# Input projection of a hybrid decoder block: weight groups of 512 columns in a ring of one group, in place of 256 columns in a ring of two

## Chip, cores and metric
One Trainium2 chip; the kernel runs on one of its cores. The metric is the device time of one execution in microseconds (us), lower is better.

## What is computed
A decoder block for 2,048 tokens of width 1,024, all in float32: a mixer (two attention groups fed by one input projection), cross-attention into 256 memory rows, a mixture of 16 experts, and a last norm. Only the input projection and what reads it matter here:

```python
# h = rms_norm(x, mix_norm): (1, 2048, 1024); w_in: (1024, 3096)
fq, fk, fv, ff, gq, gk, gv, gg, ga = jnp.split(h @ w_in, offsets, axis=-1)
# widths         512 512 512  8  256 256 512 512 16
fox = forgetting_attention(fq, fk, fv, ff + b_forget)         # 8 heads x 64
log_a = log_sigmoid(ga @ w_alpha_up + b_alpha) / 16
gla = gla_chunked(gq, gk, gv, log_a)                          # 4 heads, chunks of 64 tokens
gla = rms_norm(gla) * silu(gg)
y = concat(rms_norm(fox), gla) @ w_out
```

## The kernel before
**Precision.** A product of float32 operands is three matmuls of float32r parts: `split` (lines 64 to 72) makes a high part on ACT (line 68, or line 71 with a scale) and a low part on DVE (line 69 or 72), and `mm3` (lines 88 to 92) runs high by high (L90), high by low (L91) and low by high (L92) into one PSUM bank.

**Stage 1** (`stage1`, lines 129 to 290). The tokens are four chunks of 512. `prenorm` loads and normalises a chunk, `turn` transposes it on PE (L205) and splits it into xh and xl, which stay in SBUF for the whole stage. The columns of w_in are taken in groups. `group` (lines 140 to 148) loads a group in 8 parts (one for each 128 of the 1,024 rows) through the staging tile w1s, a ring of 4, and splits each, scaled by mix_norm, into w1r, a ring of 16: two groups of 256 columns. Two kinds of product use a group:

- `ttype` (lines 159 to 167), the transposed product: 128 columns of the group stand in the array, 512 tokens of a chunk move. 8 parts by 3 matmuls fill one bank, which is evacuated by ACT and DVE in turn (`evac`, L155 and L157) and stored by SP (L167).
- `ntype` (lines 169 to 180), the token-major product: 128 tokens stand, the group's 256 columns move. 8 parts by 3 matmuls, evacuated by `evac` or, for GG, by ACT with Silu (L179), and stored by SP (L180).

Both draw on the tile ps_mm (three banks) and on the output tile o1 (two buffers). The groups come in this order: GQ and GK (two groups, transposed, lines 234 to 264, chunk by chunk, with the transposition of the next chunk and a narrow product of 24 matmuls, `narrow`, at each chunk's end); GG and GV (two groups each, token-major, 16 token tiles to a group, lines 266 to 271); FV (two groups, token-major) and FQ, FK (two groups each, transposed, four heads to a group), in the generator `rest` (lines 273 to 287). The steps of `rest` are interleaved with those of the GLA recurrence (`gla`, lines 328 to 454), half a step of GLA per unit of main work (`interleave`, lines 34 to 44): a tile counts 2.6 units when token-major and 5.2 when transposed.

**Order of the work.** The program is written as above, but the order on each engine is made by a scheduler when the program is built: it takes what is ready by its own estimate of times, so that matmuls of different tiles, of GLA and of the transpositions may run in another order than in the text. Each engine then runs its list strictly in order. SP's list holds both the loads and the stores of this stage.

**After stage 1.** `stage2` (lines 457 to 640) is the forgetting attention, head by head. `prep` (lines 468 to 491) loads a head's queries (L474), keys (L475), running sums cr (L477) and values (L482) from DRAM, for head 0 through POOL's queue, and splits queries and keys (ACT L486 and L489, DVE L487, POOL L490); `scores` starts with L506 on PE. Its tiles take SBUF space that stage 1 used, and each waits for the tiles it covers. Stage 3a later loads w_xq with `load_w` (lines 643 to 650): 8 parts of 128 rows by 512 columns through wst, a ring of 2, split in the same way.

Of the kernel before, what the change touches and what calls it, by code (L numbers as in the profile page):

```python
# [33 lines left out]
def interleave(main, side, ratio):  # L34
    """emits side's steps among main's, `ratio` of side's per unit of main's; then what is left"""
    due, live = 0.0, True
    for w in main:
        due += w * ratio
        while live and due > 0:
            step = next(side, None)  # L40
            live = step is not None
            due -= step or 0.0
    for _ in side:
        pass


def skip(gen, n):
    """gen, after n empty steps"""
    for _ in range(n):
        yield  # L50
    yield from gen


class Trunk:
# [9 lines left out]
    def split(self, hi, lo, src, scale=None):  # L64
        """hi + lo = src (* scale), each exact in a float32r"""
# [8 lines left out]
    def rstd(self, out, ss, mul, pool, eps=EPS, tag=""):  # L74
        """out = (ss * mul + eps) ** -0.5"""
# [19 lines left out]
    def consts(self):  # L95
# [8 lines left out]
        # -1e30 above the diagonal (row q, column k > q)  # L104
# [5 lines left out]
        with self.tc.tile_pool(name="vrows", bufs=1) as rp, self.tc.tile_pool(name="ps_c", bufs=1, space=PSUM) as pp:  # L110
# [10 lines left out]
            # blank lists for the routing  # L121
# [7 lines left out]
    def stage1(self):  # L129
# [3 lines left out]
        with tc.tile_pool(name="xT", bufs=1) as xp, tc.tile_pool(name="w1", bufs=2) as wp, \  # L133
                tc.tile_pool(name="ps1", bufs=2, space=PSUM) as pp:
            xh, xl = zip(*[[xp.tile([128, KT, 512], F32R, name=f"x{n}{c}") for n in "hl"] for c in range(4)])
            # the narrow columns: forget logits at 0..7, GLA gate inputs at 32..47
# [3 lines left out]
            def group(c0):  # L140
                ws = []
                for k in range(KT):
                    st = wp.tile([128, 256], F32, name="w1s", bufs=4)
                    nc.sync.dma_start(st, w_in[k * 128:(k + 1) * 128, c0:c0 + 256])
                    w = wp.tile([128, 2, 256], F32R, name="w1r", bufs=16)
# [13 lines left out]
            def ttype(ws, m, c, dst):  # L159
                """rows m*128.. of the group's transposed product, tokens of chunk c"""  # L160
# [8 lines left out]
            def ntype(ws, i, dst, func=None):  # L169
                c, j = divmod(i, 4)  # L170
                ps = pp.tile([128, 256], F32, name="ps_mm", bufs=3)
# [3 lines left out]
                o = wp.tile([128, 256], F32, tag="o1", name="o1", bufs=2)  # L175
# [6 lines left out]
            with tc.tile_pool(name="xin", bufs=2) as ip, tc.tile_pool(name="psx1", bufs=2, space=PSUM) as px:  # L182
                xn = [[] for _ in range(4)]

                def prenorm(c):
                    """load and normalise chunk c"""
# [11 lines left out]
                def turn(c):  # L198
                    """chunk c transposed: yields after each bank"""
# [10 lines left out]
                def narrow(c):  # L210
# [6 lines left out]
                    # c: the running sum of log sigmoid(forget logit)  # L217
# [16 lines left out]
                gq, gk = group(GQ), group(GK)  # L234
                prenorm(1)
                for c in range(4):
                    cs = slice(c * 512, (c + 1) * 512)
                    tn = turn(c + 1) if c < 3 else iter(())
                    for m in range(2):
                        for n, ws in enumerate((gq, gk)):  # L240
                            ttype(ws, m, c, self.gqk_d[m, n, :, cs])
                            for _ in range(2):
                                next(tn, None)
                            if (c, m, n) == (0, 0, 0):
                                z = ip.tile([128, 8 * S // 128 + 1, 5], I32, name="zl", bufs=1)
                                nc.gpsimd.memset(z, 0)
                                # a blank entry's token is past the end in the fourth column
# [18 lines left out]
            for c0, dst in ((GG, self.gg_d), (GV, self.gv_d)):  # L266
                for g in range(2):
                    ws = group(c0 + g * 256)
                    for i in range(NT):
                        ntype(ws, i, dst[i * 128:(i + 1) * 128, g * 256:(g + 1) * 256],  # L270
                              AF.Silu if c0 == GG else None)

            def rest():
                for g in range(2):
                    ws = group(FV + g * 256)
                    for i in range(NT):
                        ntype(ws, i, self.fv_d[i * 128:(i + 1) * 128, g * 256:(g + 1) * 256])
                        yield 2.6
                for b, c0 in ((0, FQ), (8, FK)):
                    for g in range(2):  # L280
                        ws = group(c0 + g * 256)
                        for c in range(4):
                            for m in range(2):
                                h = b + 4 * g + 2 * m
                                dst = self.fqk_d[h:h + 2, :, c * 512:(c + 1) * 512].rearrange("h d s -> (h d) s")
                                ttype(ws, m, c, dst)
                                yield 5.2
# [6 lines left out]
    def gla_masks(self):  # L294
        nc, c = self.nc, self.cpool
        # GLA: of a 64-token chunk, which (key s, query t) a level of blocks of 2h settles:
        # s in a block's first half, t in its second; 0: s <= t within blocks of 8
# [30 lines left out]
    def gla(self, gp, pp):  # L328
# [19 lines left out]
        for g in range(S // G):  # L348
# [3 lines left out]
            for p in range(2):  # L352
# [9 lines left out]
                # log decay, summed within chunks (16 times the reference's, taken off in the exps)  # L362
# [29 lines left out]
                # scores within chunks, level by level  # L392
# [13 lines left out]
                # within blocks of 8: factors of both signs about the block's middle, bounded as each  # L406
                # step's decay is held at exp(-17), under a float32's resolution beside the diagonal
# [10 lines left out]
                # between the halves of blocks of 2h, about the first half's end  # L418
# [28 lines left out]
                # the queries' factor 1/8 is in here: (o / 8) / sqrt(mean(o^2) / 64 + eps)  # L447
# [9 lines left out]
    def stage2(self):  # L457
        nc, tc = self.nc, self.tc
        with tc.tile_pool(name="fx", bufs=1, reuse_waits="tile") as fp, \
                tc.tile_pool(name="psx", bufs=2, space=PSUM, reuse_waits="tile") as pp:  # L460
            vs, heads, n_evac = {}, {}, [0]
            # in the order in which the last head lets go of them, for the stage that follows
# [5 lines left out]
            def prep(h):  # L468
# [9 lines left out]
                # [q hi; q lo] over 8 against [k hi; k hi] and [k lo; k lo]  # L478
# [14 lines left out]
            def scores(u):  # L493
                """exp(s - max) of head h's query block, and its sums: yields after each bank"""
# [26 lines left out]
            def values(u0, u1):  # L521
                """the outputs of two query blocks, transposed, in the array's two column halves:
                yields after each bank"""
# [1082 lines left out]
```

## Time and profile before

| | |
|---|---|
| runs | 2484.33, 2485.76, 2489.12 us |
| median | 2485.76 us |
| span of the profiled execution, first to last instruction | 2482.5 us |
| from that span to the runs shown | 1.8 (lowest) to 6.6 us (highest) |
| PE busy | 2368.5 us (95%) |
| PEld busy (weight loads) | 2022.0 us (81%) |
| DVE, ACT, POOL busy | 1444.0, 1087.4, 451.5 us |
| mean granted clock of TensorE | 0.979 |
| matmuls | 17,849 |

The profile gives the profiled execution its span only; its own time in the sense of the runs is not listed apart, so it stands beside the runs as in the fourth line. Times within the profile count from the span's start. PE is TensorE's matmuls, PEld its weight loads, which overlap them; the duration of a matmul includes its way through the array, so that one begins before the one ahead has ended. A name such as `ps_mm<-xh,w1r` reads: the tile written, from the tiles read. `L90` is line 90; the helpers' lines (68 to 72, 90 to 92, 155, 157) serve many callers, so the tile's name tells which. In brackets stands how long the engine was idle ahead of an instruction, and who released it. SPq, POOL with DMA_DIRECT2D, and so on are transfers being issued.

### The profile page before, as it was taken

Reading aid. Unit: us, or ns where it says so; the run is one execution under the profiler, and the core shown is the slowest. Engines: PE = TensorE matmul, PEld = TensorE weight load, DVE = VectorE, ACT = ScalarE, POOL = GpSimd, SP = SyncE. Lnnn points to the kernel's source line nnn. Section 1 sums busy time; section 2 is a strip of 40 time slices with the busy share of each in tenths; the row PEclk is TensorE's granted clock in tenths of the full one; section 3 lists DMA queues with packets and bytes.
Section 4 is the critical chain, followed back from the end, with each engine's and each line's share of the span. In section 5 each row is a group of like instructions: output and inputs, shape, how many; then the busy total and the mean of one; then the engine's idle time right before and its main releaser. Section 6 shows DMA issues by size and latency. Waiting matters only on the chain. (4 is left out here: it accounts for less than half of the span.)

```text
span 2482.5 us, 46191 instructions
## 1 busy us (share of the span) xinstructions
PE 2368.5 (95%) x17849; PEld 2022.0 (81%) x17849; DVE 1444.0 (58%) x4096; ACT 1087.4 (44%) x2438; POOL 451.5 (18%) x460
## 2 busy tenths in 40 slices
PE   7999999999999999999999999999599999999996
PEld 5799999877776777777778888888499989889995
DVE  5321145455447777767542236656567868768775
ACT  6322123233236666666431035544344545454542
POOL 1000012122122222211100000111323233223231
PEclk9999999999999999999999999999799999999998
DMA  5232222332274223200174421111478888879783
GB/s 174 70 93 82 71 75 88 97 92 89 74 195 103 66 72 80 66 27 10 39 260 143 140 104 45 59 53 52 152 227 258 239 274 255 255 236 270 263 246 110
DMA packets 275218, 328.99 MB, mean 133 GB/s; under 512 B 30774, under 2 KB 223088, under 8 KB 271921
## 3 DMA queue, kind: packets, MB, share of 16 engines
q1 hardware_dynamic: 243968, 223.79, 28.9%
q0 software_dynamic: 31024, 102.20, 14.1%
q8 instruction: 141, 2.31, 0.4%
q14 instruction: 85, 0.69, 0.1%
HBM read 251.88 MB, written 84.30 MB: 135 GB/s over the span
## 5 line engine op out<-in xcount | busy, mean ns | idle before, releaser
L90 PE MATMUL gu<-xTh,wer 128*128 128x288 f32 x1024 | 305.4, 303 | 0.5 <-ACT xTh L68 0.5
L91 PE MATMUL gu<-xTl,wer 128*128 128x288 f32 x1024 | 304.7, 298 | 0.0
L92 PE MATMUL gu<-xTh,wer 128*128 128x288 f32 x1024 | 303.8, 297 | 0.0
L69 DVE TENSOR_TENSOR wer<-wes,wer 128x1024 fp32r<-128x1024 f32 x192 | 232.2, 1220 | 35.3 <-ACT wer L68 34.4
L68 ACT ACTIVATE wer<-wes 128x1024 fp32r<-128x1024 f32 x192 | 197.7, 1052 | 108.8 <-PE yd L92 42.5
L90 PE MATMUL ps_mm<-w1r,xh 128*128 128x256 f32 x768 | 219.3, 286 | 0.0
L91 PE MATMUL ps_mm<-w1r,xh 128*128 128x256 f32 x768 | 218.7, 285 | 0.0
L92 PE MATMUL ps_mm<-w1r,xl 128*128 128x256 f32 x768 | 217.9, 284 | 0.0
L90 PEld LDWEIGHTS gu<-xTh,wer 128*128 128x128 f32 x1024 | 193.9, 190 | 3.7 <-ACT xTh L68 0.9
L92 PEld LDWEIGHTS gu<-xTh,wer 128*128 128x128 f32 x1024 | 194.9, 190 | 1.8
L91 PEld LDWEIGHTS gu<-xTl,wer 128*128 128x128 f32 x1024 | 194.9, 190 | 1.5
L518 ACT ACTIVATE sc<-sc,m 128x1024 f32<-128x1024 f32 (+2 forms) x192 | 170.9, 892 | 51.2 <-DVE m L515 51.0
L536 PE MATMUL pt<-ident,sc 128*128 128x128 f32 x1088 | 177.8, 289 | 7.3 <-DVE rc L556 3.7
L529 PE MATMUL po<-t,v 128*64 128x128 f32 x2176 | 178.3, 287 | 0.0
L529 PEld LDWEIGHTS po<-t,v 128*64 128x64 f32 x2176 | 124.1, 138 | 49.4 <-issue 21.7
L536 PEld LDWEIGHTS pt<-ident,sc 128*128 128x128 f32 x1088 | 126.6, 145 | 45.2 <-issue 28.3
L506 PE MATMUL ps_s<-L,R 128*128 128x512 f32 (+2 forms) x320 | 140.4, 440 | 15.8 <-DVE m L510 11.1
L90 PE MATMUL ps_mm<-xh,w1r 128*128 128x512 f32 x384 | 153.8, 403 | 0.0
L92 PE MATMUL ps_mm<-xh,w1r 128*128 128x512 f32 x384 | 153.0, 398 | 0.0
L91 PE MATMUL ps_mm<-xl,w1r 128*128 128x512 f32 x384 | 152.8, 398 | 0.0
L90 PEld LDWEIGHTS ps_mm<-w1r,xh 128*128 128x128 f32 x768 | 147.2, 192 | 3.8 <-issue 1.9
L510 DVE CUSTOM_DVE_ANT_0 sc<-ps_s,cr,m 128x512 f32<-128x512 f32 (+2 forms) x192 | 124.3, 647 | 44.4 <-PE ps_s L507 31.6
(405 smaller groups left out, 5780.3 us busy)
## 6 DMA issues: line engine op xcount, KB each, us to landing
wes<-in_w_expert_down_dram SPq DMA_DIRECT2D x64, 512.0 KB
wes<-in_w_expert_gate_dram SPq DMA_DIRECT2D x62, 512.0 KB
wes<-in_w_expert_up_dram SPq DMA_DIRECT2D x62, 512.0 KB
yr_d<-ye SPq DMA_DIRECT2D x32, 512.0 KB
w1s<-in_w_in_dram SPq DMA_DIRECT2D x96, 128.0 KB
xt<-in_x_dram SPq DMA_DIRECT2D x16, 512.0 KB
fqk_d<-o SPq DMA_DIRECT2D x32, 256.0 KB
h_d<-x POOLq DMA_DIRECT2D x16, 512.0 KB
```

The source lines that it names most:

```text
L68: nc.scalar.activation(hi, src, AF.Copy)
L69: nc.vector.tensor_tensor(lo, src, f32(hi), OP.subtract)
L90: mm(ps, ah, bh, start=start, stop=False)
L91: mm(ps, ah, bl, start=False, stop=False)
L92: mm(ps, al, bh, start=False, stop=stop)
L506: nc.tensor.matmul(ps[:, :w], R[:, qs], L1[:, ks], start=True, stop=False)
L510: nc.vector.tensor_tensor_reduce(out=sc[:, ks], in0=ps[:, :w], in1=cr[:, ks], scale=1.0, scalar=m[:, i - 1:i] if i else -3e38, op0=OP.subt ...
L518: nc.scalar.activation(sc[:, cs], sc[:, cs], AF.Exp, bias=m[:, 4:5], accum_out=u["l"][:, j:j + 1])
L529: nc.tensor.matmul(po[half * 64:half * 64 + 64], v[:, kb, d], t[:, i], start=kb == 0, stop=kb == qb + half)
L536: nc.tensor.transpose(pt[:, i], (u0, u1)[half]["P"][:, kb * 128:(kb + 1) * 128], self.ident)
```

## The change
A group becomes 512 columns wide. w1s goes from four buffers of 256 columns to two of 512, and w1r from 16 slots of 2 x 256 to 8 of 2 x 512: the same bytes, but one group. GQ and GK, which are neighbours in w_in, become one group. The token-major product moves 512 columns into a bank, so that GG, GV and FV are one group each with 16 tiles, not two with 16 each. FQ and FK are one group each, with the four pairs of heads inside the loop over the chunks. The diff also drops comments and docstrings, which are left out here.

```diff
@@ group, ntype
-                    st = wp.tile([128, 256], F32, name="w1s", bufs=4)
-                    nc.sync.dma_start(st, w_in[k * 128:(k + 1) * 128, c0:c0 + 256])
-                    w = wp.tile([128, 2, 256], F32R, name="w1r", bufs=16)
+                    st = wp.tile([128, 512], F32, name="w1s", bufs=2)
+                    nc.sync.dma_start(st, w_in[k * 128:(k + 1) * 128, c0:c0 + 512])
+                    w = wp.tile([128, 2, 512], F32R, name="w1r", bufs=8)
...
-                ps = pp.tile([128, 256], F32, name="ps_mm", bufs=3)
+                ps = pp.tile([128, 512], F32, name="ps_mm", bufs=3)
...
-                o = wp.tile([128, 256], F32, tag="o1", name="o1", bufs=2)
+                o = wp.tile([128, 512], F32, tag="o1", name="o1", bufs=2)
@@ stage1
-                gq, gk = group(GQ), group(GK)
+                gqk = group(GQ)
...
-                        for n, ws in enumerate((gq, gk)):
-                            ttype(ws, m, c, self.gqk_d[m, n, :, cs])
+                        for n in range(2):
+                            ttype(gqk, 2 * n + m, c, self.gqk_d[m, n, :, cs])
...
-                for g in range(2):
-                    ws = group(c0 + g * 256)
-                    for i in range(NT):
-                        ntype(ws, i, dst[i * 128:(i + 1) * 128, g * 256:(g + 1) * 256],
-                              AF.Silu if c0 == GG else None)
+                ws = group(c0)
+                for i in range(NT):
+                    ntype(ws, i, dst[i * 128:(i + 1) * 128], AF.Silu if c0 == GG else None)
@@ rest
-                for g in range(2):
-                    ws = group(FV + g * 256)
-                    for i in range(NT):
-                        ntype(ws, i, self.fv_d[i * 128:(i + 1) * 128, g * 256:(g + 1) * 256])
-                        yield 2.6
+                ws = group(FV)
+                for i in range(NT):
+                    ntype(ws, i, self.fv_d[i * 128:(i + 1) * 128])
+                    yield 5.2
                 for b, c0 in ((0, FQ), (8, FK)):
-                    for g in range(2):
-                        ws = group(c0 + g * 256)
-                        for c in range(4):
-                            for m in range(2):
-                                h = b + 4 * g + 2 * m
+                    ws = group(c0)
+                    for c in range(4):
+                        for m in range(4):
+                            h = b + 2 * m
```

## Rows read from the trace of the kernel before

**Rows 1.** Busy time of each engine in six stretches (us from the span's start): GQ and GK; GG and GV; FV beside GLA; FQ and FK beside GLA; the step to the attention. Columns: the stretch, its length, busy us (and instructions) of PE, PEld, DVE, ACT and POOL, the granted clock, the DMA share and GB/s.
```profile
22.97:145.00 122.03, 122.03 (x575) 95.29 (x575) 54.87 (x130) 51.46 (x116) 0.00 (x0) 1.00 0.33 100
145.00:331.00 186.00, 186.00 (x1549) 185.74 (x1548) 28.82 (x88) 34.30 (x81) 0.18 (x1) 1.00 0.24 74
331.00:467.00 136.00, 136.00 (x1503) 124.44 (x1502) 76.08 (x194) 48.53 (x167) 31.47 (x36) 1.00 0.30 87
467.00:724.00 257.00, 257.00 (x2109) 199.13 (x2107) 126.88 (x338) 84.36 (x295) 53.53 (x78) 1.00 0.35 103
724.00:728.00 4.00, 0.08 (x1) 0.00 (x0) 3.81 (x14) 0.00 (x0) 2.99 (x3) 1.00 0.89 322
728.00:732.00 4.00, 3.26 (x13) 2.38 (x13) 3.87 (x13) 0.98 (x4) 0.00 (x0) 0.50 0.60 223
```

**Rows 2.** Who PE waited for: us in total, times, the longest. The first row is the whole answer for 20 to 330 us, the second that for 330 to 740 us.
```profile
PE pt_x L205 <- DVE xl L69: 1.7, 2, 0.9
...
PE ps_s L506 <- DVE R L487: 4.7, 1, 4.7
```

**Rows 3.** The token-major matmuls of high by high, from the view of the tile ps_mm: count, shortest, median and longest duration in ns, first and last start.
```profile
L90 PE MATMUL ps_mm<-w1r,xh x768: 278/283/388, 145.7 to 467.5; 128*128 128x256 f32 x192
```

**Rows 4.** ACT's timeline in GG: start, duration, instruction. The first two and the last two of thirteen evacuations in a row.
```profile
200.61 0.39 ACT L179 ACTIVATE o<-ps_mm 128x256 f32<-128x256 f32 x1 [2.49 <-PE ps_mm L92]
203.49 0.39 ACT L179 ACTIVATE o<-ps_mm 128x256 f32<-128x256 f32 x1 [2.49 <-PE ps_mm L92]
...
232.29 0.39 ACT L179 ACTIVATE o<-ps_mm 128x256 f32<-128x256 f32 x1 [2.49 <-PE ps_mm L92]
235.17 0.39 ACT L179 ACTIVATE o<-ps_mm 128x256 f32<-128x256 f32 x1 [2.49 <-PE ps_mm L92]
```

**Rows 5.** Timeline of DVE and ACT at the end of FK, where nothing else is on PE: the evacuations of the last three tiles of stage 1.
```profile
713.24 0.69 DVE L157 COPY o<-ps_mm 128x512 f32<-128x512 f32 x1 [5.86 <-PE ps_mm L92]
...
718.73 0.60 ACT L155 ACTIVATE o<-ps_mm 128x512 f32<-128x512 f32 x1 [10.33 <-PE ps_mm L92]
...
724.12 0.69 DVE L157 COPY o<-ps_mm 128x512 f32<-128x512 f32 x1 [10.19 <-PE ps_mm L92]
```

**Rows 6.** Timeline at the change between two groups of GV: SP issues the second half of a group's parts, and ACT splits all eight.
```profile
282.62 1.76 SPq L144 DMA_DIRECT2D w1s<-in_w_in_dram  x4
...
281.56 1.71 ACT L71 ACTIVATE w1r<-w1s,vcols 128x256 fp32r<-128x256 f32 x4
284.73 1.55 ACT L71 ACTIVATE w1r<-w1s,vcols 128x256 fp32r<-128x256 f32 x3 [1.46 <-DMA w1s<-in_w_in_dram]
286.64 0.51 ACT L71 ACTIVATE w1r<-w1s,vcols 128x256 fp32r<-128x256 f32 x1 [0.37 <-DMA w1s<-in_w_in_dram]
```

**Rows 7.** The splits' durations by shape, from the views of lines 71 and 72: count, shortest, median and longest in ns, first and last start. w1r is the projection's (256 columns), wqh and wql are w_xq's (512 columns).
```profile
L71 ACT ACTIVATE w1r<-w1s,vcols x96: 492/508/536, 13.0 to 599.8; 128x256 fp32r<-128x256 f32 x96
L71 ACT ACTIVATE wqh<-wst,vcols x8: 721/724/724, 1274.3 to 1289.9; 128x512 fp32r<-128x512 f32 x8
...
L72 DVE SCALAR_TENSOR_TENSOR w1r<-w1s,vcols,w1r x96: 472/483/1121, 14.1 to 602.0; 128x256 fp32r<-128x256 f32 x96
L72 DVE SCALAR_TENSOR_TENSOR wql<-wst,vcols,wqh x8: 743/750/753, 1275.1 to 1290.7; 128x512 fp32r<-128x512 f32 x8
```

**Rows 8.** Timeline of the load of w_xq: two issues on SP, the first split on ACT, the two splits that those issues released, and the last split on DVE.
```profile
1275.86 0.33 SPq L648 DMA_DIRECT2D wst<-in_w_xq_dram  x1
1276.76 0.38 SPq L648 DMA_DIRECT2D wst<-in_w_xq_dram  x1
...
1274.33 0.72 ACT L71 ACTIVATE wqh<-wst,vcols 128x512 fp32r<-128x512 f32 x1 [4.00 <-DMA wst<-in_w_xq_dram]
1278.41 0.72 ACT L71 ACTIVATE wqh<-wst,vcols 128x512 fp32r<-128x512 f32 x1 [1.75 <-DMA wst<-in_w_xq_dram]
1280.83 0.72 ACT L71 ACTIVATE wqh<-wst,vcols 128x512 fp32r<-128x512 f32 x1 [1.69 <-DMA wst<-in_w_xq_dram]
...
1290.69 0.75 DVE L72 SCALAR_TENSOR_TENSOR wql<-wst,vcols,wqh 128x512 fp32r<-128x512 f32 x1 [0.64 <-ACT wqh L71]
```

**Rows 9.** PE's timeline in the first group, some of whose parts are still being loaded: six matmuls of ps_mm behind four transpositions.
```profile
28.73 0.60 PE L205 MATMUL pt_x<-ident,xt 128*128 128x128 f32 x4
29.08 0.48 PE L91 MATMUL ps_mm<-xl,w1r 128*128 128x512 f32 x1
29.40 0.40 PE L92 MATMUL ps_mm<-xh,w1r 128*128 128x512 f32 x1
29.63 0.40 PE L91 MATMUL ps_mm<-xl,w1r 128*128 128x512 f32 x1
29.86 0.40 PE L92 MATMUL ps_mm<-xh,w1r 128*128 128x512 f32 x1
30.10 0.62 PE L90 MATMUL ps_mm<-xh,w1r 128*128 128x512 f32 x2
```

**Rows 10.** The step from stage 1 to the attention. POOL's timeline: the loads of head 0's keys and sums, and what they waited for. SP's waits: the longest for a store of fqk_d ahead of a load. PE's timeline: the first scores.
```profile
701.81 0.53 POOL L475 DMA_DIRECT2D k<-fqk_d  x1 [8.41 <-PE ps_mm L92]
713.50 0.56 POOL L477 DMA_DIRECT2D cr<-c_d  x1 [10.15 <-PE ps_mm L92]
...
SPq L477 <- DMA fqk_d<-o: 3.5, 1, 3.5
...
728.74 1.09 PE L506 MATMUL ps_s<-L,R 128*128 128x128 f32 x3 [4.65 <-DVE R L487]
```

More of the change, by code (lines that the diff above doesn't have):

```diff
@@ L266, in stage1 @@
             for c0, dst in ((GG, self.gg_d), (GV, self.gv_d)):
-                for g in range(2):
-                    ws = group(c0 + g * 256)
-                    for i in range(NT):
-                        ntype(ws, i, dst[i * 128:(i + 1) * 128, g * 256:(g + 1) * 256],
-                              AF.Silu if c0 == GG else None)
-            def rest():
-                for g in range(2):
-                    ws = group(FV + g * 256)
-                    for i in range(NT):
-                        ntype(ws, i, self.fv_d[i * 128:(i + 1) * 128, g * 256:(g + 1) * 256])
-                        yield 2.6
-                for b, c0 in ((0, FQ), (8, FK)):
-                    for g in range(2):
-                        ws = group(c0 + g * 256)
-                        for c in range(4):
-                            for m in range(2):
-                                h = b + 4 * g + 2 * m
-                                dst = self.fqk_d[h:h + 2, :, c * 512:(c + 1) * 512].rearrange("h d s -> (h d) s")
-                                ttype(ws, m, c, dst)
-                                yield 5.2
+                ws = group(c0)
+                for i in range(NT):
+                    ntype(ws, i, dst[i * 128:(i + 1) * 128], AF.Silu if c0 == GG else None)
+            def rest():
+                ws = group(FV)
+                for i in range(NT):
+                    ntype(ws, i, self.fv_d[i * 128:(i + 1) * 128])
+                    yield 5.2
+                for b, c0 in ((0, FQ), (8, FK)):
+                    ws = group(c0)
+                    for c in range(4):
+                        for m in range(4):
+                            h = b + 2 * m
+                            dst = self.fqk_d[h:h + 2, :, c * 512:(c + 1) * 512].rearrange("h d s -> (h d) s")
+                            ttype(ws, m, c, dst)
+                            yield 5.2
             with tc.tile_pool(name="gla", bufs=2) as gp, tc.tile_pool(name="psg", bufs=1, space=PSUM) as gpp:
```

## The prediction
> **What bounds the kernel now.** I read the page's clock row first, then the busy time by stage, then PE's own waits, then the loads at a change of group. By stage [rows 1]: from 22.97 to 724 us PE is busy all the time at a granted clock of 1.00, while DVE and ACT are at or under 56% and DMA at 24 to 35%. PE waited for somebody else for 1.7 us in one half of this stretch and 4.7 us in the other, and those 4.7 lie behind the last product [rows 2]. So every ns of PE work that goes is a ns off the stage, unless a wait takes its place. In 145 to 331 us PEld is full as well (185.74 of 186): there only the 256-column products run, one weight load of 128x128 to each. Matmul durations can't price this, since they overlap (283 ns each where a new one starts every 120 [rows 3]); I use the distance between evacuations.
>
> **Fewer, wider matmuls (the gain).** A token-major tile of 256 columns is 24 matmuls (8 parts by 3); twelve evacuations of such tiles from 200.61 to 235.17 lie 34.56/12 = 2.88 us apart [rows 4], 120.0 ns a matmul. A tile of 512 columns is 24 matmuls too: the last three evacuations, alone on PE, span (724.12 - 713.24)/2 = 5.44 us a tile [rows 5], 226.7 ns a matmul. These are the transposed products, but of the same size: 128x128 stationary, 512 columns moving, same type. The change turns two tiles of 2.88 into one of 5.44 and saves 0.32 us; GG, GV and FV have 16 token tiles each: 48 x 0.32 = 15.4 us. Put otherwise, 1,152 of 2,304 matmuls go, and each took 13.3 ns beside its columns. Had the new shape the cadence of the old columns (240 ns), the gain would be 0; the row for the same size says 226.7, and I take it. GQ, GK, FQ, FK keep their matmuls.
>
> A page of the Trainium skill would give another size (TensorE: Matmul & The Clock Gate, section Back-to-back issue gap): there a matmul takes its columns over 2.4 GHz plus 2.5 ns, which is 109 and 216 ns; that halving would save only about 2.9 us, an estimate from the page. The rows disagree with it by 11 ns in both shapes and go into the sum.
>
> **The ring of one group (the cost).** Now w1r holds 16 half-wide parts, two groups: at 281.56 us parts are split for a group that PE reaches a whole group (46 us) later. After, 8 parts of 512 are one group: part k of the next group can be split only when the last tile has read part k. There are five such changes: GQK to GG, GG to GV, GV to FV, FV to FQ, FQ to FK.
>
> The time of one refill. A split of 512 columns takes ACT 0.72 and then DVE 0.75 [rows 7]. A 128 KB part is usable 2.1 to 2.6 us after its issue now (282.62 to 284.73 for the first of four; the fourth, near 284.05, at 286.64) [rows 6]. The change moves 256 KB each through a ring of two (w1s). The kernel already has that load: w_xq, same shape, same ring, where a part was usable 2.55 us (1275.86 to 1278.41) to 4.07 us (1276.76 to 1280.83) after its issue, and the whole took from 1274.33 to 1291.44, 17.1 us [rows 8]. With the start of the group's last tile as zero: parts 0 and 1 wait staged and are done at 2.3 and 3.0; a later pair costs a landing and a split, about 4.5 us with a landing of 3.0, so pairs are done by 7.5, 11.9 and 16.4 us; with 4.07, by 8.7, 14.3 and 19.9.
>
> What hides it. The last tile runs to 5.44. If PE takes three tiles side by side (ps_mm has three banks), 0.68 us a part and tile, it has 12 x 0.68 = 8.2 us of work with four parts, to 13.6, and 12.2 with six, to 17.7. That covers 16.4 wholly and leaves about 2.3 us at the slow landing. Does the order on PE do this? The order is made by a scheduler and is not that of the text. At the start, where the first group's parts arrive late, PE runs L91, L92, L91, L92, L90 after a transposition [rows 9]; one tile alone goes L90, L91, L92, so two tiles were taken by turns, and PE waited 1.7 us in all. So I take the side-by-side order. In FV to FQ and FQ to FK PE has GLA work too: PE's matmuls apart from 32 tiles (92.2 us) filled the other 43.8 of FV's 136 us [rows 1], 2.7 us for a pair of tiles. GQK to GG has the narrow product between, 24 matmuls of 512, 5.44 us. So 0 to 2.3 us for each of the two bare changes and 0 for the three others, if the scheduler's own landing time is right; I take 3.0 us in all, and 0 to 5 as ends.
>
> If the cover goes (strictly one tile after another), a change costs 6 us (the tile would end at 17 where it ended at 10.9) to 9.5 at the slow landing; the narrow product takes 5.44 off one, GLA 2.7 off two: 18.7 to 36.6 us for the five.
>
> **Edits at nothing.** The first group: the first tile can close only when 2 MB have come, where it was 1 MB (GQ's); but all four kinds of tile can use each early part, PE has three banks for them, and the 2 MB come by the same time: 0, between -2 and +3. Splits are 48 x (0.72 + 0.75) where they were 96 x (0.51 + 0.48), evacuations half as many: less on ACT and DVE, which aren't the bound: 0. SP issues 96 fewer transfers but, with a ring of two, waits for a split before each later load, and the stores of the tiles run side by side queue behind that wait; then o1 (two buffers) holds up an evacuation, and with it one of the three banks. PE has the other two: 0, at worst 1 us a change. GLA's pace is 5.2 units a tile in place of 2 x 2.6: 0.
>
> **The hand-over to attention.** Head 0's keys were complete eight tiles before the end of stage 1; in the new order they are three tiles (16.3 us) before it. From there: evacuation 0.7, store 3.5 (SP waited that long for the last one), loads, a split and PE. Now PE stands still 4.65 us here, for DVE, and the clock is at 0.50 (1.2 GHz) for the next 4 us [rows 1, 10]. The loads had waited for SBUF space until 701.81 (keys) and 713.50 (cr) [rows 10]; x's chunks are released earlier after the change (four tiles before the end where chunk 2 had two), so cr goes ahead. I take 0; -4 (the gap closes) to +7 (keys, cr and v together).
>
> **Sum.** -15.4 + 3.0 + 0 = -12.4 us. The span of the profiled execution is 2482.5, so 2470.1; the median of three runs is 3.3 above that span, and 2485.8 - 12.4 = **2473.4 us**. A measurement of this kernel can tell about 0.2%, 5 us, from no change.
>
> **Rivals.**
> - A, strict order: the scheduler believes the parts in time and puts one tile behind the other; PE waits part by part at each change. +18.7 to +36.6 against -15.4: 2489 to 2507 us, and more if a wait lets the clock fall as at 724 us. It turns the sign once the five waits pass 15.4 us, 3.1 each. For it: nothing hides a bare change but other tiles; against: the start [rows 2, 9]. 0.16.
> - B, half a cover: two tiles side by side or a slow landing, 1.5 to 3 us a change, 10 in all: 2480 us, not to be told from no change. 0.12.
> - C, late keys: stage 1 shrinks, but PE waits 7 us more at the hand-over: 2480 us. For it: three tiles of lead in place of eight; against: three tiles are 16 us, and PE idles there already. 0.04.
> - D, the fixed share isn't per matmul: if the 512-column product cost two 256-column ones but 2.5 ns, as the matmul itself has the same columns to move, the gain is 1,152 x 2.5 ns = 2.9 us, eaten by the refills: 2486 us. Two shapes in this trace speak against it. 0.02. The page named above has this 2.5 ns.
> - The forecast, 0.66.
>
> **Range.** The forecast's own bounds are -15.4 + 0 - 4 to -15.4 + 5 + 5, 2466 to 2480. B, C and D lie in 2480 to 2486, the lower part of A up to 2492; widened by 2 us below for the start: 2464 to 2492. What is left out is A's upper half and little below, under 0.15. Faster by over 0.2%: the forecast, 0.66. Within: B, C, D, 0.18. Slower: A, 0.16.
>
> **What would show it.** Right: evacuations of GG, GV and FV 5.44 us apart; 1,152 token-major matmuls; PE's waits between 23 and 710 us under 6 us; stage 1's last product near 712. At a change, two or three evacuations close together, after a gap: tiles run side by side. Wrong: PE waiting for ACT or DVE on w1r at the five changes with single tiles behind each other (A); a cadence near 5.7 (D); PE idle for over 8 us before the first attention scores (C).

## The result, and the profile after

| | before | after |
|---|---|---|
| median (6 runs of each) | 2485.05 us | 2469.07 us (2465.42 to 2472.10) |
| ratio, 95% interval | | 0.9942 [0.9926, 0.9958] |
| span of the profiled execution | 2482.5 us | 2467.0 us |
| first product of stage 1 starts | 22.97 | 21.24 |
| first token-major product starts | 145.65 | 143.12 |
| last product of stage 1 starts | 723.70 | 703.63 |
| first scores start | 728.74 | 711.23 |
| last product of the attention starts | 1226.75 | 1211.32 |

The change is faster by 0.58%: 16.0 us between the medians, where 12.4 us and 2473.4 us were forecast. Each experiment's ratio below is to executions of the kernel before that ran beside it (medians from 2481.4 to 2483.5 us), and differences to the kernel after are those of the ratios. Two executions in a slow state (2911.38 us of the kernel before, 5970.90 us of experiment 2) are left out. The milestones (starts of matmuls in the two traces) show more than the sum: stage 1 gained 20.1 us, the attention gave 4.6 back, and the 15.4 left at its end are the 15.5 at the end of the span.

Busy time by stage, against [rows 1] (stretch, length, then busy us of PE, PEld, DVE, ACT and POOL, granted clock, DMA share, GB/s):
```profile
143.00:306.00 163.00, 163.00 (x719) 134.51 (x718) 21.84 (x62) 24.51 (x38) 0.18 (x1) 1.00 0.23 75
...
704.00:708.00 4.00, 0.01 (x1) 0.00 (x0) 3.06 (x8) 2.35 (x5) 3.00 (x3) 1.00 1.01 380
708.00:712.00 4.00, 0.77 (x3) 0.80 (x4) 3.93 (x9) 0.00 (x0) 1.93 (x2) 0.61 1.02 321
712.00:716.00 4.00, 4.00 (x17) 2.79 (x17) 3.75 (x16) 2.15 (x7) 0.00 (x0) 0.53 0.68 197
```
PE is still busy throughout GG and GV, but PEld, full before, now has 17% to spare: half as many weight loads for the same columns. Behind the last product PE stands still, and in the 4 us from 712, at the start of the attention, the granted clock is 0.53, near the lower level of 1.2 GHz. PE's waits from 20 to 715 us, the whole answer, against [rows 2] (from stage 2 on, the changed kernel's line numbers are three lower: L503 is L506 before):
```profile
PE ps_s L503 <- DVE R L484: 7.2, 1, 7.2
PE pt_x L205 <- DVE xl L69: 0.2, 1, 0.2
```
No wait for w1r at all. The token-major matmul of high by high, against [rows 3]: half as many, each of 512 columns:
```profile
L90 PE MATMUL ps_mm<-w1r,xh x384: 387/389/501, 143.1 to 440.6; 128*128 128x512 f32 x192
```
ACT's timeline at the change from GG to GV, against [rows 4, 6]: evacuations (L179 of GG, L155 of GV) and splits (L71):
```profile
219.54 0.60 ACT L179 ACTIVATE o<-ps_mm 128x512 f32<-128x512 f32 x1 [4.84 <-PE ps_mm L92]
224.98 0.60 ACT L179 ACTIVATE o<-ps_mm 128x512 f32<-128x512 f32 x1 [4.84 <-PE ps_mm L92]
225.61 1.41 ACT L71 ACTIVATE w1r<-w1s,vcols 128x512 fp32r<-128x512 f32 x2
229.85 1.57 ACT L71 ACTIVATE w1r<-w1s,vcols 128x512 fp32r<-128x512 f32 x2 [2.83 <-DMA w1s<-in_w_in_dram]
231.32 0.58 ACT L179 ACTIVATE o<-ps_mm 128x512 f32<-128x512 f32 x1
...
240.26 0.72 ACT L71 ACTIVATE w1r<-w1s,vcols 128x512 fp32r<-128x512 f32 x1 [1.01 <-DMA w1s<-in_w_in_dram]
244.87 0.60 ACT L155 ACTIVATE o<-ps_mm 128x512 f32<-128x512 f32 x1 [3.88 <-PE ps_mm L92]
247.63 0.60 ACT L155 ACTIVATE o<-ps_mm 128x512 f32<-128x512 f32 x1 [2.16 <-DMA gv_d<-o]
```
Between the two lies DVE's evacuation of the second tile, and ahead of it the last split:
```profile
241.02 0.75 DVE L72 SCALAR_TENSOR_TENSOR w1r<-w1s,vcols,w1r 128x512 fp32r<-128x512 f32 x1 [0.98 <-ACT w1r L71]
245.27 0.69 DVE L157 COPY o<-ps_mm 128x512 f32<-128x512 f32 x1 [3.50 <-PE ps_mm L92]
```
Steady tiles are 5.44 us apart. At the change comes a gap of 13.55 us and then three evacuations at 244.87, 245.27 and 247.63: three tiles were filled side by side, and from 231.32 to 247.63 are 16.31 us, just 3 x 5.44. The refill ran from 224.73, the start of GG's last tile, to 241.77: 17.0 us (17.3 at GV to FV). PE shows how close it was:
```profile
241.90 0.84 PE L90 MATMUL ps_mm<-w1r,xh 128*128 128x512 f32 x3
```
Three high-by-high matmuls in a row, one for each bank, on the last part, whose high half ACT finished at 240.98, 0.9 us earlier.

### The profile page after: what moved, and what is told of

Same layout as the page of the kernel before. It is cut to its first block, busy times and chain, and to the rows that moved or that the text cites. A ratio compares the mean times of both kernels' runs of the same rounds, so it can differ in the third digit from the quotient of the medians.

```text
span 2467.0 us, 43457 instructions
## 1 busy us (share of the span) xinstructions
PE 2348.9 (95%) x16697; PEld 1954.1 (79%) x16697; DVE 1433.0 (58%) x4032; ACT 1069.9 (43%) x2358; POOL 454.4 (18%) x460
## 5 line engine op out<-in xcount | busy, mean ns | idle before, releaser
L503 PE MATMUL ps_s<-L,R 128*128 128x512 f32 (+2 forms) x320 | 140.6, 441 | 17.6 <-DVE m L507 10.2
L507 DVE CUSTOM_DVE_ANT_0 sc<-ps_s,cr,m 128x512 f32<-128x512 f32 (+2 forms) x192 | 124.4, 648 | 45.9 <-PE ps_s L504 32.6
L91 PE MATMUL ps_mm<-w1r,xh 128*128 128x512 f32 x384 | 150.2, 393 | 0.0
L92 PE MATMUL ps_mm<-w1r,xl 128*128 128x512 f32 x384 | 149.7, 392 | 0.0
L90 PE MATMUL ps_mm<-w1r,xh 128*128 128x512 f32 x384 | 148.2, 392 | 0.0
L538 ACT ACTIVATE t<-pt 128x512 f32<-128x512 f32 (+1 forms) x192 | 103.6, 556 | 100.9 <-PE pt L533 86.4
```

The lines of the kernel that those rows point to most:

```text
L90: mm(ps, ah, bh, start=start, stop=False)
L91: mm(ps, ah, bl, start=False, stop=False)
L92: mm(ps, al, bh, start=False, stop=stop)
L503: nc.tensor.matmul(ps[:, :w], R[:, qs], L1[:, ks], start=True, stop=False)
L507: nc.vector.tensor_tensor_reduce(out=sc[:, ks], in0=ps[:, :w], in1=cr[:, ks], scale=1.0, scalar=m[:, i - 1:i] if i else -3e38, op0=OP.subt ...
L538: nc.scalar.activation(t[:, :len(todo)], pt[:, :len(todo)], AF.Copy)
```

## The experiments

**1. The width alone undone.** The ring of one 512-column group stays; all but a tile's first and last matmul are cut into two of 256 columns.
```diff
-  self.mm3(ps, xh[c][:, k, t], xl[c][:, k, t], ws[k][:, 0], ws[k][:, 1], k == 0, k == KT - 1)
+  for j, (l, r) in enumerate(((xh, 0), (xh, 1), (xl, 0))):
+      n = 512 if (k, j) in ((0, 0), (KT - 1, 2)) else 256
+      for q in range(0, 512, n):
+          nc.tensor.matmul(ps[:, q:q + n], l[c][:, k, t], ws[k][:, r, q:q + n], ...)
```


> The changed kernel, but the token-major product cut back to 256 columns: of the 24 matmuls of a tile the first and the last keep 512 columns, the 22 between become two of 256 each, with the same weight loaded twice. Groups, ring, loads, evacuations and stores stay those of the change. That is 48 x 22 = 1,056 matmuls more. Theory (a matmul costs some 13 ns beside its columns): 1,056 x 13.3 = 14.0 us slower than the changed kernel, so within 0.1% of the kernel before; evacuations in GG 5.44 + 22 x 0.0133 = 5.73 us apart. Rival 1 (the fixed share is 2.5 ns): 2.6 us slower than the changed kernel, ratio to before still about 0.995. Rival 2 (the gain came from the loads, evacuations or the start, not from the width): no slower than the changed kernel.

Measured: 2488.56 us, 1.0023 [1.0013, 1.0033]: the whole gain is gone. Two evacuations of GG on ACT (the edit moves L179 to L182 and the matmul to L177):
```profile
185.19 0.60 ACT L182 ACTIVATE o<-ps_mm 128x512 f32<-128x512 f32 x1 [5.13 <-PE ps_mm L177]
190.92 0.60 ACT L182 ACTIVATE o<-ps_mm 128x512 f32<-128x512 f32 x1 [5.13 <-PE ps_mm L177]
```
5.73 us apart, 5.44 + 22 x 0.0133 to the digit. The total is larger than expected: from the first token-major product to the last product it takes 18.2 us more than the kernel after, where 1,056 x 13.3 ns is 14.0. The rest goes with another count: between first GLA work and last product PE leaves the products for GLA 105 times, and 88 in the kernel after.

**2. The same in quarters** (128 in place of 256 in the edit above), to see whether the 13.3 ns go with every matmul.

> The kernel after, with 22 of the 24 matmuls of each token-major tile cut into four of 128 columns: 48 x 22 x 3 = 3,168 matmuls more, the same columns. Theory (each matmul of this kind costs its columns at 2.4 GHz and 13.3 ns): 4 x (53.3 + 13.3) = 266.7 ns in place of 226.7, evacuations of GG and GV 5.44 + 22 x 0.040 = 6.32 us apart, and 42 us more than the kernel after, about 1.011 of the time before. Rival (2.5 ns a matmul): 5.61 us apart, 8 us more. Rival (each matmul loads 128x128 weights anew, and a load takes about as long as the 120 ns of the narrow products in the kernel before): 4 x 120 = 480 ns, 11.0 us a tile, 267 us more.

Measured: 2704.72 us (median of three), 1.0894 [1.0870, 1.0919], some 236 us over the kernel after. The theory of the 42 us fell; the third case is the nearest. ACT's timeline in GG, and busy time in the same stretch:
```profile
196.20 0.60 ACT L182 ACTIVATE o<-ps_mm 128x512 f32<-128x512 f32 x1 [9.69 <-PE ps_mm L177]
206.49 0.60 ACT L182 ACTIVATE o<-ps_mm 128x512 f32<-128x512 f32 x1 [9.69 <-PE ps_mm L177]
```
```profile
160.00:260.00 100.00, 100.00 (x876) 99.09 (x876) 1.37 (x8) 6.00 (x10) 0.00 (x0) 1.00 0.10 35
```
A tile takes 10.29 us. Less two matmuls of 226.7 ns, 88 narrow ones share 9.84 us: 111.8 ns each, for 53 ns of columns, with PEld full. So the columns and 13.3 ns no longer set the pace. That weight loads do is an inference: PEld was full at 120.0 ns a matmul too [rows 1], so that share alone doesn't tell the two apart, and no run changed the loads alone. The 111.8 also show that a matmul with its load can go faster than the 120.0 ns at 256 columns, so loads alone don't set those. The Trainium skill (TensorE: Matmul & The Clock Gate, section LDWEIGHTS) gives columns over 1.2 GHz for one load, by which 128 columns would take 106.7 ns, an estimate from that page; the trace's 111.8 lies 5.1 ns above it.

**3. Strict order.** Every product pinned to program order, so that no tile starts before the one ahead is done.
```diff
+        if pin:
+            mm = lambda *i, **k: self.tc.keep_in_program_order(self.nc.tensor.matmul(*i, **k))
...
```
Both kinds of product call it with pin=True; the narrow product stays free.

> The changed kernel, but the matmuls of the projection's products (transposed and token-major) are held in the order of the text, so that a tile is finished before the next begins. Theory (three tiles side by side hide the refill of the ring): PE waits part by part at the changes of group. A refill took 16.8 us from the start of the last tile in the changed kernel's trace, so the next tile ends near 17.3 where it would end at 10.9: 6.4 us at GG to GV and GV to FV each, 1 at GQK to GG, 3.7 at FV to FQ and at FQ to FK: about 21 us slower than the changed kernel, ratio to before about 1.002, and a few us at the start, where the first parts are late too. Rival (the refill is hidden by staging and by the last tile itself): under 3 us slower, no waits of PE at the changes.

Measured: 2533.53 us, 1.0205 [1.0191, 1.0218], some 65 us over the kernel after, where about 21 were expected. At GG to GV the evacuations of three tiles start at 232.96, 244.74 and 250.77: 11.78 us to the first tile of GV, 6.3 over the cadence, and at GV to FV 12.22 (6.8 over). Part of PE's waits from 140 to 765 us:
```profile
PE kt L387 <- POOL kh L383: 22.0, 5, 6.8
PE ps_mm L91 <- ACT w1r L71: 7.4, 10, 1.6
PE ps_mm L91 <- DVE w1r L72: 4.3, 7, 1.8
```
The bare changes cost what the prediction's strict order said, 6 to 9.5 us. Most of the loss is another: pinning also lets GLA in less often (45 times), and GLA's own waits, 22.0 us in the first row, lie open. From 143 to 765 us PE is idle for 44.6 us, and the granted clock is 0.95 up to 478 us and 0.94 behind it, where the kernel after has 1.00 and no idle time. So this run prices the two bare changes, not the five.

**4. Two banks in place of three** (ps_mm with two buffers).

> The changed kernel with two PSUM banks for ps_mm in place of three. Theory (PE takes as many tiles side by side as there are banks): with two tiles the parts ready at 2.9, 7.3, 12.7 and 16.8 us after the last tile's start leave PE waiting about 2 us at each of the two bare changes (GG to GV, GV to FV), 0 to 2 at the others and at the start: 4 to 8 us slower than the changed kernel. Evacuations at these changes come in pairs, not in threes. Rival (the cover does not depend on the banks): no difference over 2 us. If evacuations can't be hidden with two banks, every tile gains some 0.7 us and the kernel is some 50 us slower: then it tells nothing.

Measured: 2487.65 us, 1.0017 [1.0008, 1.0026], 18.6 us over the kernel after. At GG to GV the evacuations come as a pair (245.28 and 245.71), and from 233.99 to the third at 251.77 are 17.8 us, 1.5 over three tiles; PE waits for w1r there and elsewhere:
```profile
PE ps_mm L90 <- ACT w1r L71: 4.2, 5, 1.7
```
So two tiles side by side hide all but 1.5 us of this change and 2.5 of the next (323.35 to 342.15, 18.8 us in place of 16.3). The 18.6 are more than that and than the 4 to 8 expected: 2.7 lie ahead of the first token-major product, PE waits 2.8 us for an evacuation to free a bank, and in the GLA stretch it changes to GLA 97 times in place of 88. The rest stays open.

**5. A refill twice as long** (one staging buffer w1s in place of two).

> The kernel after, with one staging buffer for the weight parts in place of two: no part can be requested before the split of the one ahead, so that a refill takes 2.3 + 7 x 4.5 = about 34 us in place of 16.8. Theory (a refill is hidden by three tiles side by side and by no more): three tiles have 16.3 us of work; the last of them ends about 36 us after the last tile's start where it ended at 21.8, so 14 us of waits on w1r at GG to GV and at GV to FV each, some less at the three changes with other work, and some at the start: 45 to 70 us more than the kernel after. Rival (the refill is far from the bound, and the side-by-side order only shows a scheduler's estimate): under 10 us more. Theory's sign in the trace: still three evacuations close together at a change, with a gap of about 30 us ahead of them in place of 13.6.

Measured: 2518.75 us, 1.0146 [1.0123, 1.0169], about 50 us more, within the 45 to 70 (two executions). PE at GG to GV:
```profile
255.20 0.96 PE L90 MATMUL ps_mm<-w1r,xh 128*128 128x512 f32 x3 [1.75 <-ACT w1r L71]
...
259.36 0.97 PE L90 MATMUL ps_mm<-w1r,xh 128*128 128x512 f32 x3 [1.73 <-ACT w1r L71]
```
A part every 4.2 us, nine matmuls on it (three tiles), then a wait. From 246.37 to the third evacuation, 276.32, are 29.95 us, 13.6 over three tiles; expected were 14. The refill ran from 240.61 to 272.62, 32.0 us. Three tiles side by side are the cover, and they cover about 16 us beyond the last tile.

**6. Head 0's keys early.** The order of FQ and FK as before, four heads at a time over all chunks.
```diff
-                    for c in range(4):
-                        for m in range(4):
+                    for c, m in [(c, 2 * g + m) for g in range(2) for c in range(4) for m in range(2)]:
+                        if True:
                             h = b + 2 * m
```


> The changed kernel, but within FQ and FK the tiles of the first four heads come ahead of those of the last four, as in the kernel before, out of the one group of 512. Theory (the gap ahead of the first attention scores grew from 4.65 to 7.2 us because head 0's keys come late, three tiles ahead of the end, and the second half of its queries waits behind them in POOL's queue): the keys are there eight tiles ahead, the gap falls back to 4 to 5 us, and the kernel gains about 2.5 us on the changed one, ratio to before about 0.993. Rival (the gap is made by DVE's constants ahead of the split of the queries, which POOL's split of the keys slows): the gap stays at 7 us as long as POOL's four splits of the keys still run beside these constants.

Measured: 2463.33 us, 0.9927 [0.9913, 0.9940], 3.7 us under the kernel after. The hand-over in the kernel after, against [rows 10]: POOL's load of the keys and its split of them; DVE's last evacuation, three of the routing's constants and the copy R; PE's first scores:
```profile
691.29 0.53 POOL L472 DMA_DIRECT2D k<-fqk_d  x1 [17.51 <-DMA fqk_d<-o]
705.00 4.93 POOL L487 TENSOR_TENSOR L<-k,L 128x512 fp32r<-128x512 f32 x4 [9.28 <-ACT L L486]
...
704.94 0.69 DVE L157 COPY o<-ps_mm 128x512 f32<-128x512 f32 x1 [11.08 <-DMA fqk_d<-o]
706.47 1.07 DVE L1035 TENSOR_TENSOR same<-ident 128x32 f32<-128x32 f32 x1
707.58 1.18 DVE L1037 TENSOR_TENSOR same<-same,ident 128x32 f32<-128x32 f32 x1
708.79 1.19 DVE L1037 TENSOR_TENSOR same<-same,ident 128x32 f32<-128x32 f32 x1
710.40 1.90 DVE L484 SCALAR_TENSOR_TENSOR R<-q,R 64x512 fp32r<-64x512 f32 x3
...
711.23 1.09 PE L503 MATMUL ps_s<-L,R 128*128 128x128 f32 x3 [7.22 <-DVE R L484]
```
The same with the keys early:
```profile
680.64 0.53 POOL L472 DMA_DIRECT2D k<-fqk_d  x1 [6.25 <-PE ps_mm L92]
702.73 4.97 POOL L487 TENSOR_TENSOR L<-k,L 128x512 fp32r<-128x512 f32 x4 [5.61 <-ACT L L486]
...
704.85 0.69 DVE L157 COPY o<-ps_mm 128x512 f32<-128x512 f32 x1 [10.19 <-PE ps_mm L92]
706.70 1.06 DVE L1035 TENSOR_TENSOR same<-ident 128x32 f32<-128x32 f32 x1
707.80 0.19 DVE L1037 TENSOR_TENSOR same<-same,ident 128x32 f32<-128x32 f32 x1
708.02 0.19 DVE L1037 TENSOR_TENSOR same<-same,ident 128x32 f32<-128x32 f32 x1
708.63 2.50 DVE L484 SCALAR_TENSOR_TENSOR R<-q,R 64x512 fp32r<-64x512 f32 x4
...
709.46 0.75 PE L503 MATMUL ps_s<-L,R 128*128 128x128 f32 x3 [4.66 <-DVE R L484]
```
The keys are loaded when fqk_d's store has landed (`<-DMA fqk_d<-o`), 10.7 us later than with the keys early. The first scores wait for R and not for them: POOL's split of them slides onto DVE's constants, and a 128x32 addition takes 1.18 us beside it and 0.19 behind it. The additions wait rather than run slowly: the three end at 707.54, 708.76 and 709.98, each 0.05 us behind the end of one of POOL's four pieces (707.49, 708.71, 709.93), while the evacuation, a copy out of PSUM that ran beside the first piece, took its usual 0.69. From the last evacuation's end to R are 4.8 us against 3.1. That is 1.7 of the 2.56 us between the two waits; the other 0.9 is the last evacuation, which follows the last product by 1.3 us and not 0.4, since its output buffer waits for a store. The Trainium skill (GPSIMD Engine Reference, section Specifications) says that GpSimd shares its SBUF interfaces with VectorE and contends with instructions of two SBUF inputs; the trace agrees, with these 1.18 and 0.19 us.

Experiment 2 keeps the late order, but there POOL's split happens to start 1.7 us ahead of the last product and not 1.4 behind it. The additions take 0.19 and the wait is short (L506 is L503 above, L487 is L484), but DVE then waits for the split of head 0's later queries:
```profile
946.86 1.09 PE L506 MATMUL ps_s<-L,R 128*128 128x128 f32 x3 [4.61 <-DVE R L487]
...
962.50 0.69 DVE L487 SCALAR_TENSOR_TENSOR R<-q,R 64x512 fp32r<-64x512 f32 x1 [6.04 <-ACT R L486]
```
From the last product to the attention's last product are 510.2 us there, 507.7 in the kernel after and 503.9 with the keys early. So the overlap explains the longer first wait, and not all that the late order costs.

**7 and 8. The routing's constants moved in program order,** behind the attention: alone, and with 6.
```diff
-                self.route_init(self.rp)
...
                         self.stage2()
+                    self.route_init(self.rp)
```


> The kernel after, with the constants of the routing (some twenty small instructions on DVE, 705.57 to 710.40 us in the trace of the kernel after) put behind the attention in program order. Theory (the hand-over's stall is DVE's: the copy R that the first scores need stands behind those constants in DVE's list): PE's wait ahead of the first scores falls from 7.2 to 2 to 3 us and the kernel gains 4 to 5 us against the kernel after (0.9942 to about 0.9923 of the time before). Rival (the stall is the keys': the last store of fqk_d, then the load, arrive too late whatever DVE does): the wait stays at 6 to 7 us and the time is that of the kernel after. Second rival: the constants cost the same where they now stand: the wait is short and the end is no earlier.

> The kernel after, with both edits at the hand-over: head 0's keys complete eight tiles before the end of stage 1 as in the kernel before, and the routing's constants behind the attention. With the order of the keys alone PE still waited 4.7 us there, for DVE. Theory (two causes, one behind the other: the keys' way through DRAM, then DVE's constants): the wait falls to 1 to 2 us and the time is 2.5 to 3.5 us below that of the order of the keys alone, about 0.9913 of the time before. Rival (one cause, the constants; the keys only decided when they run): the same time as with the constants alone moved. Rival (loads of SBUF-bound tiles set the start): the wait stays near 4.7 and nothing is gained.

Measured: 2469.17 us, 0.9949 [0.9932, 0.9965], and 2462.92 us, 0.9925 [0.9910, 0.9940]. The edit did not reach the engine: the scheduler put the constants where they had been, R starting at 710.59 in the one and 708.86 in the other, with waits of 7.1 and 4.7 us. Nothing follows for the constants; the two are near repeats of the kernel after and of experiment 6.

**9 to 11. The constants ahead of stage 1,** in another pool, all but two memsets: alone, with 6, and the kernel after again.
```diff
+    def route_consts(self):
+        nc, c = self.nc, self.cpool
...
+            self.route_consts()
             if "1" in stages:
                 self.stage1()
```


> The kernel after, with the routing's constants but for two memsets made ahead of stage 1, in the pool of constants, so that the scheduler can't put them at the hand-over. (With the same instructions only moved in program order it had put them there again: 705.36 to 710.59 us on DVE.) Theory (PE's wait of 7.2 us is DVE's constants): behind the last evacuation (705.6) DVE is free for R, ACT and POOL have the keys' parts by 706.3, so the wait falls to 2 to 3 us, and the time by 4 to 5 us against the kernel after of the same call, to about 2464. Rival (the late load of queries and keys holds the rest of head 0 as well): the wait falls, but PE waits again within the first head for the second half of its keys, and the gain is 0 to 2 us.

> The kernel after, with the keys of head 0 complete eight tiles before the end of stage 1 and the routing's constants ahead of stage 1. Theory (DVE's constants are what is left of the wait once the keys are early): the wait falls from 4.7 to 1 to 2 us, and the time by 2.5 to 3.5 us below the order of the keys alone, to about 2460. If the keys' order and the constants were the same cause, this run ends with the constants alone (2464); if the two add, below both.

> The kernel after, unchanged, beside the two others on the same chip: 0.994 of the time before, 2469 us; the wait ahead of the first scores 7.2 us, with DVE's constants between 705.4 and 710.6.

Measured: 2468.38 us, 0.9946 [0.9930, 0.9961]; 2464.09 us, 0.9928 [0.9911, 0.9944]; 2467.50 us, 0.9936 [0.9921, 0.9952]. With the constants gone the first scores come at 708.11, 3.1 us earlier than in the kernel after (PE's wait is 3.4 us), and nothing is gained at the end, where 4 to 5 us were expected. With the keys early as well the wait falls from 4.7 to 2.4, and the time is that of experiment 6, not the expected 2460. The repeat waits 8.2 us, not 7.2. DVE, POOL and PE in the first of the three:
```profile
706.66 6.34 DVE L484 SCALAR_TENSOR_TENSOR R<-q,R 64x512 fp32r<-64x512 f32 x4
...
706.15 6.30 POOL L487 TENSOR_TENSOR L<-k,L 128x512 fp32r<-128x512 f32 x4 [9.74 <-ACT L L486]
...
713.38 0.79 PE L503 MATMUL ps_s<-L,R 128*128 128x512 f32 x1 [2.93 <-DVE m L507]
```
R now runs beside POOL's split: 6.34 us for what took 2.50 alone, and the split is longer too. DVE comes to its next work (L507) so much later, and PE waits 2.9 us a few matmuls on. The wait moved. The theory that the constants were the stall fell as far as the time goes. A second possible cause beside DVE's loss to POOL is the granted clock (the last column but two). 25 us from the first scores on, in the kernel after and in the first of the three:
```profile
711.00:736.00 25.00, 21.86 (x148) 15.82 (x150) 21.36 (x74) 16.88 (x40) 6.10 (x6) 0.91 0.77 197
708.00:733.00 25.00, 20.35 (x116) 14.77 (x116) 20.67 (x59) 13.23 (x31) 7.03 (x7) 0.74 0.78 212
```
With the keys early it is 0.93, and 0.86 with the constants gone too. From the first scores to the attention's last product the first of the three takes 4.7 us more than the kernel after; a clock lower by 0.17 over 25 us can be up to 4.3 of them, an estimate. The runs don't separate the two.

Taken together, the four kernels with the changed order of FQ and FK stand at 0.9942, 0.9949, 0.9946 and 0.9936, the three with the keys early at 0.9927, 0.9925 and 0.9928. The single intervals overlap, but over all executions the means are 2468.6 us (24) and 2464.0 us (17), 4.6 us apart, with a 95% interval of about 2.9 to 6.3. The fastest version is the change with head 0's keys early, at 2463 us.

## Why the prediction was right, and where its sizes were off

- **Wider matmuls, -15.4: right.** 5.44 us a tile was read off the transposed products and holds for the token-major ones; 256 columns in the changed kernel bring 5.73 (experiment 1). D, a fixed share of 2.5 ns, would make that undoing 2.6 us and the cadence 5.50; it is excluded. That weight loads alone set the 120 ns at 256 columns is excluded by experiment 2, where as many loads a matmul went at 111.8.
- **The refill, +3.0 within 0 to 5: mechanism right, size 0.** 16.4 us were worked out, 17.0 and 17.3 measured, with 2.6 us from issue to landing in the median of the 48 loads. Three tiles side by side cover it whole. A's price for a bare change (6 us) was right too, as 6.3 and 6.8 in experiment 3; its condition, strict order, did not hold. (By its own terms the lower end of A, 18.7, is 19.2: five times 6, less 5.44 and twice 2.7.)
- **The start, 0 within -2 to +3:** the first product came 1.7 us earlier and GQ with GK took 0.8 less, -2.5 in all. In the repeat (experiment 11) it is 1.3 earlier and nothing less, and in the other variants the first product lies at 21.4 to 22.3, so much of this is scatter.
- **The hand-over, 0 within -4 to +7: the step that was mis-sized.** From the last product to the end of the attention are 507.69 us, 507.69 again in the repeat and 506.11 in experiment 7, and 503.05 before: +3.1 to +4.6. Of the 4.6, 2.6 lie ahead of the first scores and 2.0 within the attention. With the keys early it is 503.88 (504.27 in experiment 8, 503.73 in 10), while the kernels with the late order have 505.4 to 510.2: C's lead of three tiles was the cause. The prediction had reasoned that cr would go ahead; its load was issued 10.8 us ahead of the last product in place of 10.2, but the keys', which waited for the store, 12.3 ahead in place of 21.9. The longer first wait comes from where POOL's split falls on DVE's work, not from keys that PE waits for; by what way the late order costs time within the attention stays open.
- **Not foreseen, -2.2:** from the first token-major product to the last product 17.5 us went, 2.2 more than the 15.4 for the width. In this stretch PE changes from products to GLA 88 times and not 100. By this difference such a change costs about 0.2 us (2.2 over 12), by experiment 1 about 0.24 (4.1 over 17), by experiment 2 about 0.25 (4.1 of 236.9 us over 16, the rest being 48 x 4.85); an estimate, since no run changed that count alone.

The sum by these: -15.4 + 0 - 2.5 - 2.2 + 4.6 = -15.5, against -12.4. The 3.0 of refill that weren't needed are the difference; the other three nearly cancel, which is luck: none of them was forecast, and one is in large part scatter.

## What to carry to other kernels

Price a change of a matmul's width by the distance between evacuations of each shape in the same trace, and measure a width before going to it: the 13.3 ns beside the columns held at 512 and 256 columns and not at 128, and full weight loads didn't announce it. A ring of one group costs nothing as long as the engine that drains it has independent outputs enough for one refill (17.0 us here; three banks hold 16.3 us of work, beside the 5.4 of the tile that still runs). And when an order changes, follow its last product into the next stage: a late load can cost time through which engine it makes run beside which other.

## What the runs showed of the hardware

At a granted clock of 1.00 (2.4 GHz) a float32r matmul with its own 128x128 weight load starts every 226.7 ns at 512 columns and every 120.0 at 256, which is 13.3 ns beside the columns in both, but every 111.8 ns at 128: there the columns no longer set the pace, and weight loads, as inferred in experiment 2, do. DVE instructions with two SBUF inputs took longer beside POOL's tensor operation: from 0.19 to 1.18 us (128x32), and R's four pieces from 2.50 to 6.34. With PE waiting part by part in experiment 5, three matmuls in a row took 1.65 us for 0.96, and the granted clock was 0.81 over that half of the refill: a bubble cost more than its own length there.
```profile
263.53 1.65 PE L90 MATMUL ps_mm<-w1r,xh 128*128 128x512 f32 x3 [1.07 <-ACT w1r L71]
...
262.00:277.00 15.00, 12.22 (x41) 8.24 (x40) 2.94 (x4) 3.36 (x5) 0.00 (x0) 0.81 0.29 92
```
